# A two-layer decoder trunk: first x blocks on VectorE, later turns of q and k, h stored from SyncE

## The chip, the cores and the metric

The kernel runs on one core of one Trainium2 chip. The metric is the device time of one execution in microseconds (us). The engines are TensorE (PE, which multiplies), VectorE (DVE), ScalarE (ACT), GpSimd (POOL) and SyncE (SP, which here only issues transfers). ACT and POOL issue transfers too.

## The reference

Two layers of a decoder trunk for one sequence of 1024 positions and width 1024, in float32. Cut to what matters:

```python
proj = x @ w_in                      # 4864 columns
u_pool, q, k, v, xc, gate_b, gate_c, gate_logits = split(proj)
o_a = multiscale_pool_mixer(u_pool)                    # windows 2/4/8/16
q, k = apply_partial_rope(q, cos, sin), apply_partial_rope(k, cos, sin)
o_b = sliding_window_gqa_sinks(q, k, v, sinks)         # window 128
o_c = gate_b * causal_dwconv(gate_c * xc, conv_w)
merged = sum(sigmoid(gates[i]) * (o_i @ w_branch_i))
x = layer_norm(ALPHA * x + merged @ w_o)
up = causal_dwconv(x @ w_up, ffn_conv_w); a, b = split(up)
h = silu(a) * b                                        # 2816 columns
x = layer_norm(ALPHA * x + h @ w_down)
```

The rotary part turns the first 16 of each 64 head channels: x1*cos - x2*sin and x2*cos + x1*sin. cos and sin come from `positions`, the same for both layers.

## The kernel before

Every float32 product is made of three reduced-precision ones: a value is split into a high part (a cast, L90, on ACT) and the remainder (a subtraction, L94, on DVE or POOL), and `product` (L110, L111, L112) adds high x high, high x low and low x high in a PSUM bank. On top of that, matrices are cut into 2 x 2 blocks and multiplied with seven block products instead of eight, so differences of blocks of x and of the weights are needed.

A layer goes through four stages. `project` makes 19 **pairs** of column tiles of `w_in`: 12 of gate logits, and kv, two of q, two for the gated convolution, its second gate, and the pooled input. `merge` does attention and the branches, `output` the product with `w_o` and a norm. The **up** stage (`feed_forward`) makes 22 pairs of `w_up`; `activated` turns each into h and, for every odd f, makes the seven h blocks that the down product needs from the last two tiles (L790 to L793, POOL) and stores them to DRAM by seven transfers of 256 KB (L796, through `store`, L664, issued by POOL). `down` runs seven steps (A11, A12, S2, S1, S3, S4, A22) over 11 blocks j each, adds the results to y, norms the rows, and in the last layer writes them to `out`.

A `pair` has two parts. Its `begin` loads w0, runs two block products, and copies the first out of its bank (`u`, L700, ACT); its `rest` loads w1, makes weight differences on POOL (L713, L710), splits them, and runs five more products, with copies and additions between (T2's copy L724, T1's copy L728, DVE's L703, L730, L733, L735). Then it calls its `then`, the column's own work. `run_pairs` calls begin, `due`, rest for each pair in turn. `todo` is the list of pieces that wait for a pair's number (`due`), `pend` a list of pieces called by `pending`.

The first pair's x blocks are made in `first_loads`; its `rest` (L229) makes the differences T1 to T4 and the remainders, some on DVE and some on POOL. The rope angles go through DRAM: `rope_tables` writes rows (L177), `rope_spread` (L180) clears two tables, fills them from the rows, and writes them to DRAM (L192, L193), and `load_tables` (L926) loads them in each layer. `rotate` turns a tile: a copy on ACT (L339), four small transfers that ACT issues (L341, L342), three DVE operations (L343 to L345), and then `parts` splits it (L92, L94), all at once when the pair ends.

SP's and PE's instructions run in the order in which the code is written; on the other engines a scheduler orders them. An engine takes its instructions strictly in order, so a waiting one holds back those behind it. Tiles rotate through a few buffers by tag: X 14, t 6, s 3, pt 3, q 1, ql 1, ws 3, w 6.

Of the kernel before, what the change touches and what calls it, by code (L numbers as in the profile page):

```python
# [60 lines left out]
class Trunk:  # L61
# [118 lines left out]
    def rope_spread(self):  # L180
        nc, rows = self.nc, self.rows
        cos = self.new([P, S], F32, "t")
        sin = self.new([P, S], F32, "t")
        nc.vector.memset(cos, 1.0)
        nc.vector.memset(sin, 0.0)
        for base in (0, 64):
            for half in range(2):
                lo = base + 8 * half
                nc.sync.dma_start(cos[lo:lo + 8, :], rows[0])
                nc.sync.dma_start(sin[lo:lo + 8, :], rows[2 - half])  # L190
        self.tables = self.dram.tile([2, P, S], F32, name="rope_tables")
        nc.sync.dma_start(self.tables[0], cos[:])  # L192
        nc.sync.dma_start(self.tables[1], sin[:])  # L193

# [6 lines left out]
    def first_loads(self):  # L201
# [27 lines left out]
        def rest():  # L229
            self.new_blocks(("T2", "T1", "T3", "T4"))  # L230
            for j in range(2):
                x("B12", 0, 1, ("t", "q"), j)
                x("B22", 1, 1, ("t", "w"), j)
            put = lambda b, j, s, e: self.split(self.xc[b][0][:, 2 * j:2 * j + 2], self.xc[b][1][:, 2 * j:2 * j + 2],
                                                s, "scalar", e)
            g = lambda n, j: f[n, j][:]
            t1 = {}
            for j in range(2):
                t1[j] = self.new([P, 2, HALF], F32, "w")
                nc.vector.tensor_tensor(t1[j][:], g("B12", j), g("B11", j), op=ALU.subtract)  # L240
                nc.gpsimd.tensor_tensor(g("B12", j), g("B22", j), g("B12", j), op=ALU.subtract)
                nc.vector.tensor_tensor(g("B11", j), g("B22", j), t1[j][:], op=ALU.subtract)
                put("T2", j, g("B11", j), "vector")
                put("T1", j, t1[j][:], "gpsimd")
            for j in range(2):
                put("T3", j, g("B12", j), "vector")
            self.new_blocks(("B22",))
            for j in range(2):
                nc.vector.tensor_tensor(g("B21", j), g("B11", j), g("B21", j), op=ALU.subtract)
                put("T4", j, g("B21", j), "vector")  # L250
                put("B22", j, g("B22", j), "gpsimd")

# [82 lines left out]
    def rotate(self, c, cos, sin):  # L335
# [9 lines left out]
        nc.vector.tensor_tensor(c[:], c[:], swp[:], op=ALU.add)  # L345
        return self.parts(swp, c)

    def parts(self, hi, c):

        hi, lo = hi[:].bitcast(F32R), c[:].bitcast(F32R)  # L350
        self.split(hi, lo, c[:], "vector", "gpsimd")
        return hi, lo
# [16 lines left out]

    def project(self, l, tables, first):  # L370

        nc = self.nc
        st = {}

        def kv(k, v):
            st["tab"] = tables()
            hi, lo = self.rotate(k, *st["tab"])
            for n in range(2):
                own, other = slice(64 * n, 64 * n + 64), slice(64 - 64 * n, P - 64 * n)
                self.store(self.kd[n, own], hi[own])  # L380
                self.store(self.kd[n, other], lo[own])

# [10 lines left out]

            self.todo.append((self.pairs + 1, keys_first))

        def qq(i):
            def then(*c):
                for j in range(2):
                    for n, x in enumerate(self.rotate(c[j], *st["tab"])):
                        self.store(self.qd[:, :, n, 2 * i + j, :].rearrange("b c q -> c b q"),  # L400
                                   x.rearrange("c (b q) -> c b q", q=P))
            return then
# [16 lines left out]
        def gate_b(*c):  # L419
            for i in range(2):  # L420
                nc.vector.tensor_tensor(c[i][:], c[i][:], st["y", i][:], op=ALU.mult)
                operand(i, st["y", i], c[i])

        def pooled(*c):
            for i in range(2):
# [12 lines left out]

                self.todo.append((self.pairs + 2 + i, mapped))

# [6 lines left out]

        gates = [gate(n) for n in range(12)]
        thens = gates[:2] + [kv, qq(0), qq(1), gates[2], gated_conv(0), gated_conv(1), gate_b, gates[3], pooled] + gates[4:]
        made, second = first or (None, None)  # L450
        if second:
            self.pend.append(lambda: None)
            self.pend.append(lambda: (second(), self.parameters()))
            self.todo.append((1, self.rope_spread))
# [201 lines left out]
    def made(self, src, e_lo="vector"):  # L656
# [3 lines left out]
        return t[:, 0, :], t[:, 1, :]  # L660

    def store(self, dst, src):

        self.nc.gpsimd.dma_start(dst, src if src.dtype == F32 else src.bitcast(F32))  # L664

    def pair(self, srcs, parity, then, made=None):
# [38 lines left out]
        def rest():  # L705
            a, (ca, cb), u = st["a"], st["c"], st["u"]
            a11, a12 = st["w0"][:, lo], st["w0"][:, hi]
            w1 = load(1)
            a21, a22 = w1[:, lo], w1[:, hi]
            sub = lambda out, x, y: nc.gpsimd.tensor_tensor(out, x, y, op=ALU.subtract)  # L710
            s1 = self.new([P, HALF], F32, "ql")
# [52 lines left out]
    def activated(self, l, f, ca, cb):  # L764
# [30 lines left out]
        for name, src in blocks:  # L795
            self.store(four(self.hs[STATIONARY.index(name), f // 2]), src)  # L796

    def down(self, l):
# [78 lines left out]
        for n, (name, banks, fresh, closes, reads) in enumerate(plan):  # L877
            if n == 5:
                g, b = self.gains(l, 1)
            held = []  # L880
            for j in range(NJ):
                late = n == 6 and j >= NJ - (LATE if last else 6)
                ops = operands(n, name, j, late)
# [21 lines left out]
    def finish(self, l, t, y, g, b):  # L905
# [7 lines left out]
        elif t == 7:  # L913
            out = lambda cs: (nc.sync if cs.start else nc.scalar).dma_start(self.out[t, :, cs], z[:, cs])
            self.norm(z, g, b, "halves", None, out)
        else:
            self.norm(z, g, b, "vector")
            nc.sync.dma_start(self.out[t], z[:])

# [6 lines left out]
    def load_tables(self):  # L926
        cos, sin = self.new([P, S], F32, "q"), self.new([P, S], F32, "pt")
        self.nc.sync.dma_start(cos[:], self.tables[0])
        self.nc.sync.dma_start(sin[:], self.tables[1])
        return cos, sin  # L930

    def run(self):
        self.pend, self.todo, self.pairs = [], [], 0
        self.spill = self.dram.tile([8, P, D], F32, name="spill")
# [7 lines left out]
        with self.tc.manual_schedule(engines={mybir.EngineType.SP, mybir.EngineType.PE}):  # L942
# [10 lines left out]
            self.constants()  # L953
            self.rope_tables()
            for l in range(DEPTH):
                self.project(l, self.load_tables, first if l == 0 else None)
                self.merge(l)
# [18 lines left out]
def lay_out(inp):  # L976
# [10 lines left out]
    for l in range(DEPTH):  # L987
# [5 lines left out]
        gt = ac + [gbb[:, e * 256:(e + 1) * 256] for e in range(4)]  # L993
        win.append(column_tiles(np.concatenate([*gt[:2], k, v, q[:, heads], gt[2], *conv, gb, gt[3], u, *gt[4:]], axis=1)))
        a = column_tiles(inp["w_branch_a"][l])
# [45 lines left out]
```

## Time and profile before

| | |
|---|---|
| median of 3 runs | 2927.76 us (2921.65 to 3175.77) |
| the profiled execution | 2920.5 us, span 2918.7 us |
| busy: PE, DVE, POOL, ACT | 2614.4, 1974.0, 1552.7, 1196.5 us |
| mean granted clock of PE | 0.951 |
| moved by DMA | 390.64 MB, mean 134 GB/s |
| PE busy from 0 to 73, 73 to 146, 146 to 219 us | 34.90, 53.78, 56.00 us |

The profile is one execution on the chip. Rows of the timeline give start, duration, engine, line of the kernel, operation, output <- input and, in brackets, how long the engine was idle before and what ended that. Rows of waits give the waiting engine, tile and line, what it waited for, the sum in us, the number of times and the longest. SPq and ACTq are instructions that issue transfers.

### The profile page before, as it was taken

What the parts mean: (1) busy time and instruction counts of PE and PEld (TensorE: products, weight loads), DVE (VectorE), ACT (ScalarE), POOL (GpSimd) and SP (SyncE); (2) the same over time, 40 slices, a digit from 0 to 9 for tenths busy, and PEclk for the clock granted to TensorE, in tenths of its full rate; (3) what the DMA queues carried; (4) which work ended last, traced back from release to release, by engine and by line L of the source; (5) the groups of instructions that cost most, each with busy time, mean ns of one, the idle gap of its engine ahead of it and who ended that gap; (6) DMA issues with size and microseconds to landing.
All of it is one profiled execution on the core that took longest, in us unless ns stands there. A gap on an engine that the chain in (4) does not pass through costs nothing.

```text
span 2918.7 us, 31980 instructions
## 1 busy us (share of the span) xinstructions
PE 2614.4 (90%) x11408; PEld 2113.4 (72%) x11408; DVE 1974.0 (68%) x2285; ACT 1196.5 (41%) x1987; POOL 1552.7 (53%) x1103
## 2 busy tenths in 40 slices
PE   4779999999799999799689899999989999997985
PEld 3568887777677777678577788878767777776763
DVE  7476635846888888475486664377587888875754
ACT  4333444533444444334343335444344444443332
POOL 5354534766466666270644555367656666553513
PEclk7889999999999999999789999999989999998996
DMA  2342338554133222565323324665522322337533
GB/s 98 114 144 84 121 135 245 158 177 166 61 98 100 93 93 94 210 237 164 110 79 121 105 95 153 207 183 163 190 94 91 101 94 91 98 115 259 177 105 130
DMA packets 131184, 390.64 MB, mean 134 GB/s; under 512 B 17056, under 2 KB 17824, under 8 KB 130000
## 3 DMA queue, kind: packets, MB, share of 16 engines
q1 hardware_dynamic: 93872, 258.41, 27.2%
q0 software_dynamic: 25856, 90.85, 10.2%
q10 hardware_dynamic: 11296, 39.35, 3.5%
q8 instruction: 89, 1.46, 0.2%
q14 instruction: 71, 0.58, 0.1%
HBM read 282.79 MB, written 104.43 MB: 133 GB/s over the span
## 4 chain that ended last, share of the span: by engine, by line
PE 25%; DVE 20%; POOL 13%; DMA 8%; issue 7%; ACT 4%; SPq 0%; ACTq 0%; POOLq 0%; DVEq 0%
PE b L111 8%; PE b L112 8%; PE b L110 8%; POOL ws L710 5%; DVE w L94 5%; DMA ws<-in_w_up 4%; DVE q L775 4%; POOL ql L713 2%; ACT w L90 1%; DVE t L733 1%; DVE ve L274 1%; POOL X L836 1%; DMA X<-in_w_down 1%; ACT q L772 1%; PE b L297 1%
## 5 line engine op out<-in xcount | busy, mean ns | idle before, releaser
L110 PE MATMUL b<-X,w 128*128 128x512 f32 x2552 | 1020.9, 400 | 122.0 <-ACT s L700 62.5
L112 PE MATMUL b<-X,w 128*128 128x512 f32 x2552 | 1004.4, 394 | 23.5 <-DVE w L94 15.2
L111 PE MATMUL b<-X,w 128*128 128x512 f32 x2552 | 1004.1, 393 | 2.0 <-DVE X L94 2.0
L94 DVE TENSOR_TENSOR w<-ws,w 128x512 fp32r<-128x512 f32 (+1 forms) x449 | 508.4, 1135 | 321.2 <-ACT w L90 314.2
L110 PEld LDWEIGHTS b<-X,w 128*128 128x128 f32 x2552 | 485.8, 190 | 259.0 <-ACT s L700 79.8
L90 ACT CAST w<-ws 128x512 fp32r<-128x512 f32 (+1 forms) x605 | 405.8, 680 | 491.4 <-POOL ws L710 200.2
L112 PEld LDWEIGHTS b<-X,w 128*128 128x128 f32 x2552 | 485.0, 190 | 131.7 <-DVE w L94 18.1
L111 PEld LDWEIGHTS b<-X,w 128*128 128x128 f32 x2552 | 486.7, 191 | 101.0 <-DVE X L94 3.4
L94 POOL TENSOR_TENSOR w<-ws,w 128x512 fp32r<-128x512 f32 (+2 forms) x156 | 305.6, 1961 | 407.4 <-ACT w L90 404.4
L713 POOL TENSOR_TENSOR ql<-ws 128x512 f32<-128x512 f32 x82 | 119.0, 1452 | 348.6 <-DMA ws<-in_w_in 216.9
L110 PE MATMUL b<-w 128*128 128x512 f32 x528 | 209.7, 397 | 53.9 <-ACT w L90 53.9
L111 PE MATMUL b<-w,w 128*128 128x512 f32 x528 | 211.8, 401 | 26.2 <-DVE w L94 20.4
L112 PE MATMUL b<-w,w 128*128 128x512 f32 x528 | 208.5, 395 | 0.0
L94 DVE TENSOR_TENSOR w<-X,w 128x512 fp32r<-128x512 f32 (+1 forms) x106 | 111.6, 1073 | 90.3 <-ACT w L90 84.8
L775 DVE SCALAR_TENSOR_TENSOR q<-t,par,q 128x1023 f32<-128x1023 f32 x88 | 153.4, 1743 | 13.8 <-ACT q L772 13.6
L110 PEld LDWEIGHTS b<-w 128*128 128x128 f32 x528 | 101.2, 192 | 77.5 <-ACT w L90 56.0
L710 POOL TENSOR_TENSOR ws<-ws,ws 128x512 f32<-128x512 f32 x82 | 153.2, 1868 | 5.8
L111 PEld LDWEIGHTS b<-w,w 128*128 128x128 f32 x528 | 101.1, 192 | 56.8 <-DVE w L94 30.1
L775 DVE SCALAR_TENSOR_TENSOR pt<-t,par,pt 128x1023 f32<-128x1023 f32 x88 | 135.6, 1541 | 0.3
L710 POOL TENSOR_TENSOR ws<-ql,ws 128x512 f32<-128x512 f32 x82 | 128.7, 1569 | 6.3
L90 ACT CAST w<-X 128x512 fp32r<-128x512 f32 (+1 forms) x110 | 75.4, 704 | 134.9 <-PE b L112 64.4
L710 POOL TENSOR_TENSOR ws<-ws 128x512 f32<-128x512 f32 x82 | 116.2, 1417 | 14.7 <-DVE w L94 11.7
(247 smaller groups left out, 3892.6 us busy)
## 6 DMA issues: line engine op xcount, KB each, us to landing
ws<-in_w_up SPq DMA_DIRECT2D x88, 512.0 KB
ws<-in_w_in SPq DMA_DIRECT2D x75, 512.0 KB
gates<-t ACTq DMA_DIRECT2D x48, 512.0 KB
h_blocks<-t POOLq DMA_DIRECT2D x88, 256.0 KB, 2.8
ws<-in_w_o SPq DMA_DIRECT2D x40, 512.0 KB
h_blocks<-pt POOLq DMA_DIRECT2D x66, 256.0 KB, 2.7
t<-gates SPq DMA_DIRECT2D x32, 512.0 KB
t<-q_parts POOLq DMA_DIRECT2D x64, 256.0 KB, 4.4
```

Of the source, the lines that this page charges most:

```text
L90: self.nc.scalar.copy(hi, src)
L94: return eng.tensor_tensor(lo, src, hi.bitcast(F32), op=ALU.subtract)
L110: self.nc.tensor.matmul(out, wh, xh, start=start and i == 0, stop=False, skip_group_check=more)
L111: self.nc.tensor.matmul(out, wh, xl, start=False, stop=False, skip_group_check=more)
L112: self.nc.tensor.matmul(out, wl, xh, start=False, stop=stop and i == n - 1, skip_group_check=more)
L274: nc.vector.scalar_tensor_tensor(ve[:], ve[:], r[:], r[:], op0=ALU.mult, op1=ALU.mult)
L297: self.nc.tensor.transpose(ps[:, k * P:(k + 1) * P], src[:, k * P:(k + 1) * P], self.ident[:])
L710: sub = lambda out, x, y: nc.gpsimd.tensor_tensor(out, x, y, op=ALU.subtract)
L713: nc.gpsimd.tensor_tensor(s1[:], a21, a22, op=ALU.add)
L733: nc.vector.tensor_tensor(part(cb, 0), flat(v[:, 1, :]), flat(d[:]), op=ALU.subtract)
L772: nc.scalar.mul(y[:], c[:], w(2))
L775: nc.vector.scalar_tensor_tensor(y[:, d:], c[:, :S - d], w(k), y[:, d:], op0=ALU.mult, op1=ALU.add)
```

## The change

1. First x blocks: the differences for T3 and the remainders of T1 and B22, made by POOL before, are made by DVE, in another order. POOL does none of the x blocks.
2. Rope tables: `rope_spread` uses the q and pt buffers instead of two t buffers and keeps the tables there for layer 0 (`self.tab`); the copy in DRAM for layer 1 is written from POOL. In the code the call that makes the angles comes after the second load of x.
3. Columns: gate columns alternate with the others (g0, g1, kv, g2, q0, g3, q1, g4, conv0, g5, conv1, g6, gate_b, g7, pooled, g8 to g11), with the weights laid out to match. k and q are turned (`rotate`) one pair later and split and stored two pairs later; the high part is cast by ACT instead of DVE. The split of gate_b's product comes a pair later.
4. h blocks: for f below 20 the seven stores are put off to pair f + 2 and issued by SP right behind that pair's w1 load. f = 21 is stored by POOL as before; what is left of the others goes in `down`, at j = 3 of its first step.
5. Down: the pieces of `pend` come at other places in A22, and the last layer's stores of even rows go there instead of being issued at once.

```diff
 def rope_spread(self):
-    cos = self.new([P, S], F32, "t")
-    sin = self.new([P, S], F32, "t")
+    cos, sin = self.new([P, S], F32, "q"), self.new([P, S], F32, "pt")
...
-    nc.sync.dma_start(self.tables[0], cos[:])
-    nc.sync.dma_start(self.tables[1], sin[:])
+    nc.gpsimd.dma_start(self.tables[0], cos[:])
+    nc.gpsimd.dma_start(self.tables[1], sin[:])
+    self.tab = cos, sin
...
 # first_loads, rest
-    nc.gpsimd.tensor_tensor(g("B12", j), g("B22", j), g("B12", j), op=ALU.subtract)
...
-    put("T1", j, t1[j][:], "gpsimd")
+for j in range(2):
+    put("T1", j, t1[j][:], "vector")
 for j in range(2):
+    nc.vector.tensor_tensor(g("B12", j), g("B22", j), g("B12", j), op=ALU.subtract)
     put("T3", j, g("B12", j), "vector")
...
-    put("B22", j, g("B22", j), "gpsimd")
+    put("B22", j, g("B22", j), "vector")
...
 # project
+def later(n, f):
+    self.todo.append((self.pairs + n, f))
+def turn(c, put):
+    free = []
+    later(1, lambda: free.append(self.rotate(c, *self.tab)))
+    later(2, lambda: put(*self.parts(free[0], c)))
...
-thens = gates[:2] + [kv, qq(0), qq(1), gates[2], gated_conv(0), gated_conv(1), gate_b, gates[3], pooled] + gates[4:]
+others = [kv, qq(0), qq(1), gated_conv(0), gated_conv(1), gate_b, pooled]
+thens = gates[:1] + [f for i in range(7) for f in (gates[i + 1], others[i])] + gates[8:]
...
 # parts
-    self.split(hi, lo, c[:], "vector", "gpsimd")
+    self.split(hi, lo, c[:], "scalar", "gpsimd")
...
+def put_off(self, dst, src):
+    self.late.append((self.pairs + 2, dst, src))
+def flush(self, all=False):
+    for n, dst, src in [x for x in self.late if all or x[0] <= self.pairs]:
+        self.nc.sync.dma_start(dst, src)
+    self.late = [] if all else [x for x in self.late if x[0] > self.pairs]
...
 # pair, rest, behind w1's load
+    self.flush()
...
 # activated
-    self.store(four(self.hs[STATIONARY.index(name), f // 2]), src)
+    (self.put_off if f < NFF - 2 else self.store)(four(self.hs[STATIONARY.index(name), f // 2]), src)
...
 # down
+    if n == 0 and j == 3:
+        self.flush(True)
...
-    if n == 6 and j in (3, 4):
+    if n == 6 and j == 4:
         self.pending()
...
-    if held and q < 2:
-        self.pending()
+    if held and q < 3:
+        self.pending(4 if last else 1)
...
 # finish, last layer
-    nc.sync.dma_start(self.out[t], z[:])
+    put = lambda: nc.sync.dma_start(self.out[t], z[:])
+    if t % 2:
+        put()
+    else:
+        self.pend.append(put)
```

Where instructions stand now, at three places. The first is SP in the third and fourth pair of layer 0; `in_w_in` are pair loads, `rope_rows` and `rope_tables` the angles in DRAM. Before:

```order
L190 DMA t_542<-rope_rows 8x1024
L192 DMA rope_tables<-t_541 128x1024
L193 DMA rope_tables<-t_542 128x1024
L680 DMA ws_556<-in_w_in 128x1024
L928 DMA q_647<-rope_tables 128x1024
L929 DMA pt_648<-rope_tables 128x1024
L680 DMA ws_666<-in_w_in 128x1024
```

After the change, in the same place:

```order
L188 DMA q_541<-rope_rows 8x1024
L189 DMA pt_542<-rope_rows 8x1024
L704 DMA ws_556<-in_w_in 128x1024
L704 DMA ws_647<-in_w_in 128x1024
```

The four transfers of whole tables are gone from between the loads. The eight `rope_rows` stay on SP; the clears for which they wait moved on DVE from behind the work of pair 1 (L703 of t_538) to ahead of pair 1's weight remainders.

The second is ACT in the pair behind the first q column, in which q's two tiles (t_844, t_845) are turned. L340 is the copy of `rotate`, L342 and L343 its transfers, L724 the copy `u` (L700 before), L749 T2's copy (L724 before) and L753 T1's (L728 before). After the change:

```order
L342 DMA pt_983<-t_844 8x1024
L724 COPY s_966<-b_952 128x512
L343 DMA pt_983<-t_844 8x1024
L342 DMA pt_983<-t_844 8x1024
L343 DMA pt_983<-t_844 8x1024
L342 DMA pt_992<-t_845 8x1024
L753 COPY s_1050<-b_1023 128x512
L343 DMA pt_992<-t_845 8x1024
L342 DMA pt_992<-t_845 8x1024
L343 DMA pt_992<-t_845 8x1024
L90 CAST w_1020<-ws_944 128x512
L749 COPY s_966<-b_952 128x512
```

Before, the turn of the first q column stands in the pair that follows it like this:

```order
L339 COPY pt_827<-t_703 128x1024
L700 COPY s_862<-b_848 128x512
L341 DMA pt_827<-t_703 8x1024
L342 DMA pt_827<-t_703 8x1024
L341 DMA pt_827<-t_703 8x1024
L342 DMA pt_827<-t_703 8x1024
L90 CAST w_898<-ws_840 128x512
L724 COPY s_862<-b_848 128x512
```

The copy of `u` stands ahead of most of the transfers now, and T2's copy (L749) behind T1's (L753), three transfers and a cast, where before it came ahead of T1's.

The third is SP at the end of the last layer; `out` is the result, the lines with `h_blocks` and `in_w_down` are the two halves of a down operand. Before:

```order
L842 DMA X_20476<-in_w_down 128x512
L918 DMA out<-pt_19222 128x1024
L918 DMA out<-pt_19226 128x1024
L918 DMA out<-t_19230 128x1024
L918 DMA out<-t_19234 128x1024
L819 DMA s_20571<-h_blocks_15683 128x512
L845 DMA s_20571<-in_w_down 128x512
```

After:

```order
L867 DMA X_20472<-in_w_down 128x512
L844 DMA s_20563<-h_blocks_15679 128x512
L870 DMA s_20563<-in_w_down 128x512
L844 DMA ws_20583<-h_blocks_15679 128x512
L870 DMA ws_20583<-in_w_down 128x512
```

The four stores of even rows now come behind all eleven A22 operands.

More of the change, by code (lines that the diff above doesn't have):

```diff
@@ L345, in rotate @@
         nc.vector.tensor_tensor(c[:], c[:], swp[:], op=ALU.add)
-        return self.parts(swp, c)
+        return swp
     def parts(self, hi, c):
         hi, lo = hi[:].bitcast(F32R), c[:].bitcast(F32R)
-        self.split(hi, lo, c[:], "vector", "gpsimd")
+        self.split(hi, lo, c[:], "scalar", "gpsimd")
         return hi, lo
@@ L368, in windows, with project, put @@
                                        op0=ALU.mult, op1=ALU.subtract)
-    def project(self, l, tables, first):
+    def project(self, l, first):
         nc = self.nc
         st = {}
-        def kv(k, v):
[L376 to L381, printed above, removed]
+        def later(n, f):
[4 more added lines that the diff above has]
+            later(2, lambda: put(*self.parts(free[0], c)))
+        def kv(k, v):
+            if l:
+                self.load_tables()
+            def put(hi, lo):
+                for n in range(2):
+                    own, other = slice(64 * n, 64 * n + 64), slice(64 - 64 * n, P - 64 * n)
+                    self.store(self.kd[n, own], hi[own])
+                    self.store(self.kd[n, other], lo[own])
             def keys_first():
@@ L392, in keys_first @@
                     self.store(self.vd[:, :, c * HALF:(c + 1) * HALF].rearrange("a p c -> p a c"), t)
-            self.todo.append((self.pairs + 1, keys_first))
+            later(1, keys_first)
+            turn(k, put)
         def qq(i):
@@ L398, in then, with put @@
                 for j in range(2):
-                    for n, x in enumerate(self.rotate(c[j], *st["tab"])):
-                        self.store(self.qd[:, :, n, 2 * i + j, :].rearrange("b c q -> c b q"),
-                                   x.rearrange("c (b q) -> c b q", q=P))
+                    def put(*x, j=j):
+                        for n in range(2):
+                            self.store(self.qd[:, :, n, 2 * i + j, :].rearrange("b c q -> c b q"),
+                                       x[n].rearrange("c (b q) -> c b q", q=P))
+                    turn(c[j], put)
             return then
@@ L421, in gate_b @@
                 nc.vector.tensor_tensor(c[i][:], c[i][:], st["y", i][:], op=ALU.mult)
-                operand(i, st["y", i], c[i])
+                later(1, lambda i=i: operand(i, st["y", i], c[i]))
         def pooled(*c):
@@ L437, in mapped @@
                     operand(2 + i, self.new([P, S], F32, "pt"), c[i])
-                self.todo.append((self.pairs + 2 + i, mapped))
+                later(2 + i, mapped)
         def gate(n):
@@ L452, in project @@
             self.pend.append(lambda: None)
-            self.pend.append(lambda: (second(), self.parameters()))
+            self.pend.append(lambda: (second(), self.rope_tables(), self.parameters()))
             self.todo.append((1, self.rope_spread))
@@ L929, in load_tables @@
         self.nc.sync.dma_start(sin[:], self.tables[1])
-        return cos, sin
+        self.tab = cos, sin
     def run(self):
-        self.pend, self.todo, self.pairs = [], [], 0
+        self.pend, self.todo, self.late, self.pairs = [], [], [], 0
         self.spill = self.dram.tile([8, P, D], F32, name="spill")
@@ L953, in run @@
             self.constants()
-            self.rope_tables()
             for l in range(DEPTH):
-                self.project(l, self.load_tables, first if l == 0 else None)
+                self.project(l, first if l == 0 else None)
                 self.merge(l)
@@ L993, in lay_out @@
         gt = ac + [gbb[:, e * 256:(e + 1) * 256] for e in range(4)]
-        win.append(column_tiles(np.concatenate([*gt[:2], k, v, q[:, heads], gt[2], *conv, gb, gt[3], u, *gt[4:]], axis=1)))
+        qs = q[:, heads]
+        some = [np.concatenate([k, v], axis=1), qs[:, :256], qs[:, 256:], np.concatenate(conv[:2], axis=1),
+                np.concatenate(conv[2:], axis=1), gb, u]
+        mixed = gt[:1] + [m for i in range(7) for m in (gt[i + 1], some[i])] + gt[8:]
+        win.append(column_tiles(np.concatenate(mixed, axis=1)))
         a = column_tiles(inp["w_branch_a"][l])
```

## The prediction

> **What bounds the kernel now.** I read the busy totals and the clock in 40 slices first, then what TensorE (PE) waits for, then four stretches in order of time.
>
> ```profile
> PE 2614.4 (90%) x11408; PEld 2113.4 (72%) x11408; DVE 1974.0 (68%) x2285; ACT 1196.5 (41%) x1987; POOL 1552.7 (53%) x1103
> PEclk7889999999999999999789999999989999998996
> PE b L110 <- ACT w L90: 99.2, 11, 24.9
> PE b L110 <- ACT s L700: 62.5, 41, 8.0
> ```
>
> PE is the bound: 90% busy. About 304 us are not busy, so a change that leaves the matmuls alone can win only there. The two rows of waits (engine, tile, line, what it waited for: us in total, times, longest) hold half of it: few long waits for a weight's cast (L90), and 41 short ones for the copy of the first product out of its bank (L700). The change touches both. The span is 2918.7, this execution took 2920.5, and the runs shown have the median 2927.76; I sum against 2920.5 and leave 7 us of that spread to the range.
>
> **Part 1: first x blocks.** The rows are start, duration, engine, line, and in brackets the idle time before and its releaser.
>
> ```profile
> 25.95 1.22 DVE L240 TENSOR_TENSOR w<-t,pt 128x1024 f32<-128x1024 f32 x1
> 28.34 3.38 DVE L240 TENSOR_TENSOR w<-q,pt 128x1024 f32<-128x1024 f32 x1
> 39.34 2.39 DVE L150 TENSOR_SCALAR sink<-sink 128x8 f32<-128x8 f32 x2
> 46.08 2.28 DVE L94 TENSOR_TENSOR X<-pt,X 128x1024 fp32r<-128x1024 f32 x1
> 57.07 0.68 DVE L94 TENSOR_TENSOR w<-ws,w 128x512 fp32r<-128x512 f32 x1
> 57.80 0.80 PE L112 MATMUL b<-X,w 128*128 128x512 f32 x1 [8.61 <-DVE w L94]
> ```
>
> DVE does 12 large operations from 25.95 to 57.07, most at 2.28 to 3.38 us, which I put down to POOL's work on x beside it; the first takes 1.22. PE's L112 at 57.80 waits for the weight remainder that stands behind them. Afterwards DVE does 18 of them and POOL none. 18 x 1.22 = 22.0, plus the sink rows 2.4, gives 50.3; POOL's four weight subtractions (L713, L710) now fall into this time, and if each catches one DVE operation (2.28 instead of 1.22) that adds 4.2: 54.5. I take 52.5, between the ends, so L112 starts at 53: **+5 us** (+3 to +7). POOL reaches those subtractions earlier, so the 24.9 us wait ahead of this one turns partly into a longer one here; only the end counts.
>
> **Part 2: the rope rows on SyncE (SP).**
>
> ```profile
> SPq L189 <- DVE t L184: 32.7, 1, 32.7
> 92.92 0.91 DVE L184 MEMSET t<- 128x1024 f32 x1 [0.16 <-issue]
> 93.90 0.35 SPq L189 DMA_DIRECT2D t<-rope_rows  x1
> 103.99 12.20 SPq L680 DMA_DIRECT2D ws<-in_w_in  x3
> 106.50 1.26 POOL L713 TENSOR_TENSOR ql<-ws 128x512 f32<-128x512 f32 x1 [30.28 <-DMA ws<-in_w_in]
> 111.15 0.80 PE L110 MATMUL b<-X,w 128*128 128x512 f32 x1 [19.19 <-ACT w L90]
> ```
>
> SP stands 32.7 us at L189 until DVE clears the tables, which stands behind pair 1's last work on DVE; then come twelve table transfers, and the next w1 load goes at 103.99. POOL, idle since 76.2, gets it at 106.50 and PE loses 19.19. The two clears now stand ahead of pair 1's remainders on DVE (0.91 each, up to 2 us, hidden behind PE's 19 us pair; I charge 0.8), in buffers that are free, and L192, L193, L928, L929 leave SP. So SP goes on at about 60, and the load waits only for its buffer, free around POOL's 76. What is late next is nothing in this pair: **+18.4** (+15 to +21). That the angles stand behind the second load in the code counts nothing: their rows on DVE keep their place.
>
> 111.15 also shows a matmul of 0.80, and the first two slices of the clock row are 7 and 8. The Trainium skill ("TensorE: Matmul & The Clock Gate", Part 1) says that the array falls to half clock after an idle window and climbs back after steady work; by that rule some 2 us of slow steps behind the stall would go as well. The trace agrees with the slow steps; the sum leaves them out.
>
> **Part 3: turning k and q.** Rows five and six are PE's waits from 140 to 220 and from 1580 to 1660; the last is a stretch: length, PE busy (count), PEld, DVE, ACT, POOL, clock, DMA share, GB/s.
>
> ```profile
> 152.92 1.04 ACT L339 COPY pt<-t 128x1024 f32<-128x1024 f32 x1 [4.73 <-DMA k_parts<-pt]
> 153.99 0.63 ACTq L341 DMA_DIRECT2D pt<-t  x1
> 158.32 0.58 ACT L700 COPY s<-b 128x512 f32<-128x512 f32 x1
> PE b L110 <- ACT s L700: 17.0, 3, 7.4
> PE b L110 <- ACT s L700: 16.6, 3, 8.0
> 219.00:438.00 219.00, 219.00 (x968) 181.39 (x967) 119.28 (x134) 93.31 (x152) 106.19 (x78) 1.00 0.33 114
> ```
>
> Here ACT waits for a pt buffer that a store still reads, and PE's next copy L700 is queued behind. With the turn a pair later, its store two pairs later and gate columns between, the buffers are free by then, so these 33.6 us go. But in the four pairs in which q is turned (two a layer) ACT's new order sets T2's copy (L724) behind T1's (L728), three DMA issues and a cast. T3 cannot start before: 0.59 + 3 x 0.63 + 0.62 + 0.59 = 3.7 us after T1, say 4. 33.6 - 4 x 4 = **+17.6** (+5, if waits for pt come back in other pairs, to +30, if the copy in fact comes early). The extra gate's and pooled's later place: the pooled maps now fall where the projection ends, and PE is full there before (219.00 of 219.00, 968 matmuls at 0.226 us a step), so a loss is possible and a gain is not: **-2** (-8 to 0).
>
> **Part 4: storing h in the up stage.** The first row is the stretch of layer 0's up pairs.
>
> ```profile
> 781.00:1160.00 379.00, 362.04 (x1549) 287.84 (x1549) 327.44 (x280) 171.41 (x263) 245.69 (x196) 1.00 0.30 95
> 948.49 2.32 POOL L710 TENSOR_TENSOR ws<-ws,ws 128x512 f32<-128x512 f32 x1
> 968.42 2.32 POOL L710 TENSOR_TENSOR ws<-ws,ws 128x512 f32<-128x512 f32 x1
> 977.47 1.80 POOL L664 DMA_DIRECT2D h_blocks<-t  x3
> 989.40 2.32 POOL L710 TENSOR_TENSOR ws<-ws,ws 128x512 f32<-128x512 f32 x1
> 959.48 1.28 DVE L775 SCALAR_TENSOR_TENSOR q<-t,par,q 128x1023 f32<-128x1023 f32 x1 [0.62 <-ACT q L772]
> 978.20 3.48 DVE L775 SCALAR_TENSOR_TENSOR q<-t,par,q 128x1023 f32<-128x1023 f32 x1
> 962.92 1.14 ACT L90 CAST w<-ws 128x512 fp32r<-128x512 f32 x2
> 943.23 41.23 SPq L680 DMA_DIRECT2D ws<-in_w_up  x5
> ```
>
> Clock 1.00, DVE 86% busy, 17 us of PE idle in this layer. POOL's L710 starts 19.93 us after the last in one kind of pair and 20.98 in the other, the one with the store instructions. There DVE's first L775 takes 3.48 instead of 1.28 while POOL issues three of them, and the copy that frees PE's bank is late with it. Taking seven issues from POOL should make the long pairs like the short ones: 1.05 x 10 a layer x 2 = **+21**. Ends: 8, if POOL's arithmetic (L790 to L793) is what holds DVE; 35, if the short pairs shorten too (84 matmuls at 0.226 need 19.0). SP takes 7 issues of 0.3 to 0.5 us a double pair and waits most of a pair, so they are hidden unless their transfers delay the w0 load behind them (rival D). The pt buffer that is held longer is wanted by ACT's L772 only at the end of pair f+2.
>
> **Part 5: the end.**
>
> ```profile
> 2802.19 0.43 SPq L842 DMA_DIRECT2D X<-in_w_down  x1
> 2842.50 3.66 SPq L918 DMA_DIRECT2D out<-pt  x2
> 2850.07 0.41 SPq L819 DMA_DIRECT2D s<-h_blocks  x1
> 2854.59 1.26 POOL L846 TENSOR_TENSOR s<-X,s 128x512 f32<-128x512 f32 x1 [28.05 <-DMA s<-in_w_down]
> 2856.98 0.80 PE L110 MATMUL b<-w 128*128 128x512 f32 x1 [23.13 <-ACT w L90]
> 2847.26 2.36 DVE L291 TENSOR_TENSOR t<-t,t 128x1024 f32<-128x1024 f32 x2 [0.70 <-ACT t L290]
> 2891.11 0.69 DVE L860 TENSOR_TENSOR pt<-pt,b 128x512 f32<-128x512 f32 x1 [1.31 <-PE b L112]
> ```
>
> SP issues nothing from 2802 to 2842: the out stores of four rows wait for their norms, and the eleven A22 loads stand behind them. PE loses 23.13, then runs at the pace of operands made one at a time until the first row's last read at 2891.11. Now the loads stand ahead, so they land while PE still works on S4, whose end is 2856.98 - 23.5 = 2833.5. A22's three early columns need 3 x 4 x 3 x 0.226 = 8.1 us of PE, the eight held ones 5.4 for the first row: at best 2847. But DVE's norms run until 2849.6 and hold back the remainder of the third column: 2849.6 + 2.1 for it + 2.7 for its matmuls + 5.4 = 2860, say 2862. Gain 2891 - 1.3 - 2862 = **+28** (+22 with another operand 6 late; +36 if the norms give way). The three rows behind stay as they are.
>
> The end of layer 0's down stage gets its transposes in other places, and the load of y behind the last h stores stays: **+3** (-5 to +8).
>
> **Sum.** 5 + 18.4 + 17.6 - 2 + 21 + 28 + 3 = 91: 2920.5 - 91 = **2829**. All low ends together would give 2880, all high ones 2790.
>
> **Rivals.**
> A, the forecast (0.63): 2806 to 2852.
> B, more (0.12): even pairs drop towards 19.0 and the end takes its upper price: 91 + 14 + 8 gives 2807 or less, down to 2795.
> C, less (0.17): ACT's new order costs more than 4 us a place, waits for pt return in gate pairs and the norms eat half of the end: 91 - 12 - 13 - 14 gives 2868, 2853 to 2885.
> D, slower (0.06): the seven stores, 7 x 256 KB = 1.84 MB, stand on SP ahead of the next w0 load, and if the queue drains them in turn that load is late. w1 goes at 943.2 and w0's cast is due at about 962.9: 19.7 us, less eight issues of 0.4, for the stores and w0's 0.52 MB, which is 143 GB/s.
>
> ```profile
> 438.00:511.00 73.00, 66.55 (x317) 56.28 (x316) 38.04 (x79) 34.52 (x95) 33.12 (x35) 0.91 0.87 245
> h_blocks<-t POOLq DMA_DIRECT2D x88, 256.0 KB, 2.8
> ```
>
> Against it: a stretch of 73 us moves 245 GB/s. For it: one store takes 2.8 from issue to landing; seven one after another and w0, twice a store's size, are 25.2, 5.5 over, in 20 pairs 110 lost against 70 won elsewhere: 2920.5 + 110 - 70 = 2960. It decides as soon as the queue drains slower than 143 GB/s. "DMA: Bandwidth & Descriptors" of the Trainium skill (Queues, rings and completion order) says that SP's descriptors are consumed in ring order on each engine, which is the rule against this change; the trace has no store and load behind one another on SP to show it.
> E (0.02): the changed parts cancel, 2900 to 2935.
>
> **How the numbers follow.** A measurement of this kernel tells about 2% from no change, so faster means below 2869. A and B lie there, and most of C: 0.63 + 0.12 + 0.10 = 0.85. Within 2% are the rest of C, E and a mild D: 0.10. Slower 0.05. The range 2802 to 2868 leaves out half of B, a third of C, D and E: about 0.2.
>
> **What would show it.** Part 1: POOL's first L713 before 40 and PE's L112 near 53. Part 2: no wait of 32 us of SP for the clears, PE full from 60 to 150. Part 3: no L700 wait over 2 us in the projection, four waits of 4 us for L724's copy. Part 4: L710 starts near 19.9 apart in all pairs, the DVE row of 3.48 gone. Part 5: SP's A22 loads before 2833 on the old count, and DVE's first last read 28 us earlier against the end of S4. Wrong it would be if w0's cast in the up stage waits for its transfer, or if new waits for pt or s buffers stand in the gate pairs.

## The result and the profile after

The median of four runs is 2818.94 us (2816.18 to 2819.78). The kernel before took 2921.49 to 2927.76 in three runs, 2923.6 in the mean; its fourth, 3175.77, is disturbed and not part of the ratio. The ratio is 0.964, with a 95% interval of 0.9621 to 0.9659: some 105 us less, where 91 were forecast. The profiled execution took 2816.18 us, with a span of 2814.4, which is 104.3 shorter than the span before.

First the page, and the longest of PE's waits, in the kernel after the change. L724 is the copy of the first product (L700 before), L749 that of T2's product (L724 before).

```profile
PE 2596.4 (92%) x11408; PEld 2118.0 (75%) x11408; DVE 1876.6 (67%) x2273; ACT 1228.1 (44%) x2005; POOL 1466.5 (52%) x959
PEclk7989999999999999999799999999999999998998
PE b L110 <- ACT w L90: 45.2, 10, 15.8
PE b L110 <- ACT s L724: 18.5, 7, 4.4
PE b L110 <- ACT s L749: 17.5, 6, 3.5
```

The waits for a cast fell from 99.2 to 45.2 and those for the first copy from 62.5 to 18.5; a new row has come in, L749 with 17.5, which the prediction priced at four times 4 us (six such waits came, of 3.5 at most). PE has the same 11408 matmuls. DVE's busy time fell by 97 us with 12 instructions less.

**The start.** The two rows at the end are stretches: length, busy time of PE (with its matmuls), PEld (its weight loads), DVE, ACT, POOL, clock, DMA share, GB/s.

```profile
33.74 2.28 DVE L94 TENSOR_TENSOR X<-pt,X 128x1024 fp32r<-128x1024 f32 x1
49.57 1.21 DVE L94 TENSOR_TENSOR X<-w,X 128x1024 fp32r<-128x1024 f32 x1
50.71 0.23 DVE L150 TENSOR_SCALAR sink<-sink 128x8 f32<-128x8 f32 x2
51.59 0.80 PE L112 MATMUL b<-X,w 128*128 128x512 f32 x1 [11.56 <-DVE w L94]
55.09 0.35 SPq L188 DMA_DIRECT2D q<-rope_rows  x1
65.70 38.68 SPq L704 DMA_DIRECT2D ws<-in_w_in  x6
0.00:73.00 73.00, 41.25 (x157) 32.67 (x158) 47.80 (x62) 33.66 (x48) 26.90 (x35) 0.79 0.37 131
73.00:146.00 73.00, 71.15 (x317) 58.38 (x315) 33.42 (x43) 31.14 (x50) 29.84 (x25) 1.00 0.36 118
```

DVE's operations take 2.28 while POOL makes its four subtractions, and 1.21 once it is idle. PE's held L112 starts at 51.59 instead of 57.80. SP issues the rope rows from 55.09 instead of 93.90, and PE is busy for 71.15 of the second 73 us, 53.78 before, at full clock. Counted by matmuls, the one that started at 132.6 before starts at 104.5. Ahead of it one wait of 19.19 is gone, and with it slow steps: before, the ten matmuls behind that wait took 4.83 us (111.15 to 115.98, most of them 0.43 apart); the same ten now take 2.27, 0.23 apart.

**The projection.** First the waits of PE from 110 to 240, then ACT in the pair in which the first column of q is turned.

```profile
PE b L110 <- ACT s L724: 8.8, 3, 3.9
PE b L110 <- ACT s L749: 6.8, 2, 3.5
143.72 1.99 ACT L340 COPY pt<-t 128x1024 f32<-128x1024 f32 x2 [2.14 <-DVE t L760]
145.62 0.58 ACT L724 COPY s<-b 128x512 f32<-128x512 f32 x1
153.67 0.59 ACT L753 COPY s<-b 128x512 f32<-128x512 f32 x1 [7.47 <-PE b L112]
155.02 0.63 ACTq L343 DMA_DIRECT2D pt<-t  x1
155.69 0.62 ACT L90 CAST w<-ws 128x512 fp32r<-128x512 f32 x1 [1.44 <-DMA pt<-t]
156.21 0.58 ACT L749 COPY s<-b 128x512 f32<-128x512 f32 x1
```

The old waits of 17.0 for the first copy are not gone: 8.8 are left, and 6.8 have come for T2's copy. The turn's copies (L340) start as soon as q's last block is written (L760), though the code calls the turn a pair later, and L724 stands behind both.

**The up stage.** The first row is the same 379 us of layer 0's pairs; SP rows follow, then what SP waited for.

```profile
749.00:1128.00 379.00, 375.12 (x1651) 309.22 (x1650) 300.77 (x297) 189.50 (x278) 228.13 (x140) 1.00 0.34 104
886.77 2.15 POOL L735 TENSOR_TENSOR ws<-ws,ws 128x512 f32<-128x512 f32 x1
905.94 2.16 POOL L735 TENSOR_TENSOR ws<-ws,ws 128x512 f32<-128x512 f32 x1
925.55 1.63 POOL L735 TENSOR_TENSOR ws<-ws,ws 128x512 f32<-128x512 f32 x1
895.95 2.12 DVE L800 SCALAR_TENSOR_TENSOR q<-t,par,q 128x1023 f32<-128x1023 f32 x1
915.24 1.28 DVE L800 SCALAR_TENSOR_TENSOR q<-t,par,q 128x1023 f32<-128x1023 f32 x1 [0.61 <-ACT q L797]
895.73 23.59 SPq L704 DMA_DIRECT2D ws<-in_w_up  x4
919.37 6.18 SPq L683 DMA_DIRECT2D h_blocks<-pt  x3
SPq L683 <- DVE pt L804: 86.3, 20, 5.5
SPq L683 <- POOL t L815: 68.0, 18, 4.2
```

PE's idle time in this stretch fell from 17 to 4 us. Both kinds of pair are now as long as PE's own work, 38.0 us for two (SP's loads at 857.75 and 895.73). DVE's 3.48 is 2.12. And SP does not store long after h is made, though the code says two pairs later: it runs so far ahead that it stands at the stores until h (L804) and its differences (L815) are there.

**The end.** SP, DVE and PE in order of time.

```profile
2750.68 0.43 SPq L870 DMA_DIRECT2D ws<-in_w_down  x1
2775.47 1.48 SPq L945 DMA_DIRECT2D out<-pt  x2
2776.68 1.16 DVE L94 TENSOR_TENSOR w<-X,w 128x1024 fp32r<-128x1024 f32 x1
2777.90 0.80 PE L111 MATMUL b<-w,w 128*128 128x512 f32 x1 [9.19 <-DVE w L94]
2788.38 0.69 DVE L885 TENSOR_TENSOR pt<-pt,b 128x512 f32<-128x512 f32 x1 [2.80 <-PE b L112]
```

SP has all A22 operands issued by 2751, ahead of the stores to out. The wait of 23.13 is gone; 9.19 are left, for the remainder that stands behind the norms on DVE.

Where the 104 us between the two profiled executions came from, by the time of the same matmul in the two traces (us gained):

| stretch | layer 0 | layer 1 |
|---|---|---|
| start, to the end of the third pair's work | 28.1 | - |
| rest of the projection | -3.2 | -3.4 |
| merge and output product | 6.5 | 2.3 |
| up stage | 23.9 | 24.7 |
| down | 3.1 | 22.4 |

### The profile page after: what moved, and what is told of

Its sections match the earlier page's. It is cut to its first block, busy times and chain, and to the rows that moved or that the text cites. A ratio compares the mean times of both kernels' runs of the same rounds, so it can differ in the third digit from the quotient of the medians.

```text
span 2814.4 us, 31939 instructions
## 1 busy us (share of the span) xinstructions
PE 2596.4 (92%) x11408; PEld 2118.0 (75%) x11408; DVE 1876.6 (67%) x2273; ACT 1228.1 (44%) x2005; POOL 1466.5 (52%) x959
## 4 chain that ended last, share of the span: by engine, by line
PE 31%; DVE 7%; issue 4%; POOL 4%; ACT 2%; DMA 2%; SPq 0%; ACTq 0%; DVEq 0%; POOLq 0%
PE b L111 10%; PE b L112 10%; PE b L110 10%; DVE w L94 1%; DVE X L94 1%; ACT s L507 1%; DVE ve L275 1%; ACT w L90 0%; POOL ws L735 0%; POOL X L861 0%; POOL w L94 0%; ACT X L90 0%; POOL X L863 0%; DVE st L259 0%; DVE m L498 0%
## 5 line engine op out<-in xcount | busy, mean ns | idle before, releaser
L110 PE MATMUL b<-X,w 128*128 128x512 f32 x2552 | 1016.4, 398 | 56.9 <-ACT s L724 18.5
L112 PE MATMUL b<-X,w 128*128 128x512 f32 x2552 | 1009.6, 396 | 27.6 <-DVE w L94 19.3
L94 DVE TENSOR_TENSOR w<-ws,w 128x512 fp32r<-128x512 f32 (+1 forms) x449 | 466.8, 1043 | 357.4 <-ACT w L90 342.9
L112 PEld LDWEIGHTS b<-X,w 128*128 128x128 f32 x2552 | 487.9, 191 | 135.7 <-DVE w L94 22.5
L94 POOL TENSOR_TENSOR w<-ws,w 128x512 fp32r<-128x512 f32 (+1 forms) x156 | 307.4, 1973 | 427.5 <-ACT w L90 425.3
L738 POOL TENSOR_TENSOR ql<-ws 128x512 f32<-128x512 f32 x82 | 125.2, 1527 | 348.9 <-DMA ws<-in_w_in 256.5
L111 PE MATMUL b<-w,w 128*128 128x512 f32 x528 | 215.3, 408 | 37.4 <-DVE w L94 29.6
L112 PE MATMUL b<-w,w 128*128 128x512 f32 x528 | 211.6, 401 | 0.0
L735 POOL TENSOR_TENSOR ws<-ws,ws 128x512 f32<-128x512 f32 x82 | 141.8, 1729 | 5.9
L800 DVE SCALAR_TENSOR_TENSOR q<-t,par,q 128x1023 f32<-128x1023 f32 x88 | 126.8, 1441 | 16.2 <-ACT q L797 15.1
L800 DVE SCALAR_TENSOR_TENSOR pt<-t,par,pt 128x1023 f32<-128x1023 f32 x88 | 122.1, 1388 | 0.3
```

The source lines that it names most:

```text
L94: return eng.tensor_tensor(lo, src, hi.bitcast(F32), op=ALU.subtract)
L110: self.nc.tensor.matmul(out, wh, xh, start=start and i == 0, stop=False, skip_group_check=more)
L111: self.nc.tensor.matmul(out, wh, xl, start=False, stop=False, skip_group_check=more)
L112: self.nc.tensor.matmul(out, wl, xh, start=False, stop=stop and i == n - 1, skip_group_check=more)
L738: nc.gpsimd.tensor_tensor(s1[:], a21, a22, op=ALU.add)
L800: nc.vector.scalar_tensor_tensor(y[:, d:], c[:, :S - d], w(k), y[:, d:], op0=ALU.mult, op1=ALU.add)
```

## Experiments: each part undone or done alone

Each kernel was timed beside the kernel before; the ratios below are to it.

**only_h_late**: the kernel before, with `put_off`, `flush` and the lines that use them; one of these is shown.

```diff
-    self.store(four(...), src)
+    (self.put_off if f < NFF - 2 else self.store)(four(...), src)
```

> The kernel before with part 4 alone (h stores put off two pairs and issued by SP). Theory: POOL's store instructions lengthen all pairs of the up stage, and the whole gain of its two stretches, 23.9 + 24.7 = 48.6 us between the two traces, belongs to part 4: 2924.7 - 48.6 = 2876, pairs 19.0 us apart. Rival, the step on record: only the pairs with stores shorten, 21 us: 2904, pairs 19.9 apart.

Measured: 2873.79 us, ratio 0.9838 (0.9824 to 0.9853): 47 us less. The theory's 2876 holds, the 21 us on record don't. The stretch of the up pairs and the page of this kernel:

```profile
780.00:1159.00 379.00, 375.16 (x1644) 309.02 (x1643) 301.02 (x296) 189.21 (x278) 226.68 (x140) 1.00 0.33 103
PE 2602.2 (91%) x11408; PEld 2123.3 (74%) x11408; DVE 1888.8 (66%) x2285; ACT 1212.5 (42%) x1987; POOL 1483.2 (52%) x963
```

PE is full here as well, and the 140 store instructions that left POOL took 85 us of DVE's busy time with them (1974.0 to 1888.8), with the same 2285 DVE instructions.

**late_pool**: the changed kernel, with the put-off stores issued by POOL.

```diff
-    self.nc.sync.dma_start(dst, src)
+    self.nc.gpsimd.dma_start(dst, src)
```

> The changed kernel with the put-off stores issued by POOL instead of SP, at the same place of the program. Theory: it matters which engine issues them, so the up stage goes back to 20.4 us a pair and the time to 2819 + 40 to 50 = 2859 to 2869. Rival: it matters that they come late and no longer stand between the weight subtractions and the h blocks: within 8 us of 2819.

Measured: 2873.67 us, ratio 0.9843 (0.9826 to 0.9859), 55 us more than the change. The stretch of the up pairs, and POOL and DVE in one of them:

```profile
750.00:1129.00 379.00, 362.22 (x1547) 288.80 (x1546) 327.80 (x278) 170.17 (x261) 241.72 (x194) 1.00 0.30 95
905.33 1.78 POOL L683 DMA_DIRECT2D h_blocks<-t  x3
906.98 1.45 POOL L735 TENSOR_TENSOR ws<-ws 128x512 f32<-128x512 f32 x1
906.03 3.48 DVE L800 SCALAR_TENSOR_TENSOR q<-t,par,q 128x1023 f32<-128x1023 f32 x1
```

The stretch is that of the kernel before to within 0.2 us of PE, and DVE's row of 3.48 is back. The stores stand between the subtractions on POOL again, because the scheduler orders POOL. So a later place in the code wins nothing on POOL, and the gain needs another engine to issue the stores; a version with late stores on POOL in an order of one's own wasn't tried.

**early_sp**: put off by one pair.

```diff
-    self.late.append((self.pairs + 2, dst, src))
+    self.late.append((self.pairs + 1, dst, src))
```

> The changed kernel with the stores put off by one pair instead of two, still on SP. In the trace SP runs more than a pair ahead, and w0's cast is done about 14 us before PE needs it. Theory: SP takes its instructions in order, so the loads of pair f+2 now stand behind stores whose h is not made yet; w0 would be issued some 18 us later, 4 more than its lead plus its landing and splitting, about 5.5 us lost in each of 20 pairs: 2819 + 110 = 2929. Rival: SP has slack enough, since it waits most of each pair anyway: 2819.

Measured: 3012.02 us, ratio 1.0312 (1.0293 to 1.0331). This is the rival D of the prediction come true in another way: 193 us more than the change, 9.7 in each of 20 pairs, where 5.5 were expected.

SP's rows, what SP waited for, and ACT's cast of a w0:

```profile
944.61 23.49 SPq L683 DMA_DIRECT2D h_blocks<-pt  x3
968.28 3.06 SPq L683 DMA_DIRECT2D h_blocks<-t  x4
971.44 21.41 SPq L704 DMA_DIRECT2D ws<-in_w_up  x4
SPq L683 <- DVE pt L804: 428.6, 21, 22.2
975.24 0.62 ACT L90 CAST w<-ws 128x512 fp32r<-128x512 f32 x1 [3.99 <-DMA ws<-in_w_up]
```

SP stands up to 22.2 us at a store until h is made, and four loads go behind it. The late cast also stands ahead of ACT's work on h, which delays the next h: that loop is my reading of why it is more than 5.5, and it was not measured by itself. Part of the loss is the clock: it is 0.95 from 760 to 1200, in the up stage of layer 0, and 1.00 in that of the change, an estimated 22 us of these 440. One pair's difference in the program decides between 105 us won and 91 lost.

The trace also answers what the prediction left open in rival D. The w0 load that SP issues at 971.44, 0.4 us behind the last of seven stores, is cast from at 975.24: at most 3.8 us from issue to landing, against 3.4 to 3.6 for three loads of this size in the up stage of the kernel before. Six of the seven stores and the load were issued from 966.90 on and took 8.3 us up to the cast, where the sum's prices would give 6 x 2.8 + 5.6 = 22.4.

**columns_before**: part 3 undone.

```diff
...
-thens = gates[:1] + [f for i in range(7) for f in (gates[i + 1], others[i])] + gates[8:]
+thens = gates[:2] + [kv, qq(0), qq(1), gates[2], gated_conv(0), gated_conv(1), gate_b, gates[3], pooled] + gates[4:]
...
-later(1, lambda: free.append(self.rotate(c, *self.tab)))
-later(2, lambda: put(*self.parts(free[0], c)))
+put(*self.parts(self.rotate(c, *self.tab), c))
...
```

> The changed kernel with part 3 undone (columns in the old order, k and q turned and split when their pair ends). By the step on record, part 3 is worth 17.6 - 2 = 15.6 us, so undoing it gives 2834.5. By the two traces the projections lost 3.2 and 3.4 us against the old order, and the merges behind them became 6.5 and 2.3 us shorter: part 3 is worth 2 us or nothing, 2817 to 2822, and the waits for the first copy are back with 17 us in each projection.

Measured: 2820.22 us, ratio 0.9654 (0.964 to 0.9668), which cannot be told from the change's 0.964. Part 3 wins nothing that can be told (1 us by the medians, 5 by the profiled executions), not 15.6. PE's waits from 110 to 220 in this kernel:

```profile
PE b L110 <- ACT s L722: 17.4, 3, 8.2
```

17.4 against 8.8 + 6.8 after the change. The rest of the projection is 4 us shorter here and the merge with the output product 4.8 longer (297.5 against 292.7); why it gains from the new order I did not separate.

**both_urgent**: the changed kernel, with the first copy and T2's raised in priority in every pair (`urgent` tells the scheduler to put an instruction ahead; T1's copy has it already). Only ACT's order changes (and what follows from it).

```diff
-    nc.scalar.copy(u[:, 0, :], a[:])
+    with self.urgent():
+        nc.scalar.copy(u[:, 0, :], a[:])
...
-    nc.scalar.copy(u[:, 1, :], a[:])
+    with self.urgent():
+        nc.scalar.copy(u[:, 1, :], a[:])
```

> The changed kernel with the copies of the first and of T2's product (L724, L749) at the same raised priority that T1's copy has, so that in the pairs in which q is turned T2's copy stands ahead of T1's and of three transfers. Theory: the four waits of 3.5 us for it go, 14 us: 2805 to 2808. Rival: the same transfers then hold back the cast for the last product or the next pair's copy, and the time stays within 4 us of 2819.

Measured: 2800.53 us, ratio 0.9583 (0.9568 to 0.9598): 18.4 less than the change (14.9 between the profiled executions), more than the 14 of the theory. The first row is ACT, the next two are PE's waits from 110 to 240; the last two are this stretch in the changed kernel and in this one.

```profile
149.98 0.59 ACT L751 COPY s<-b 128x512 f32<-128x512 f32 x1 [3.11 <-DMA pt<-t]
PE b L112 <- DVE w L94: 6.4, 4, 2.4
PE b L110 <- ACT s L725: 2.2, 2, 1.7
110.00:240.00 130.00, 114.21 (x455) 91.59 (x454) 75.60 (x70) 49.65 (x76) 62.13 (x45) 0.91 0.39 119
110.00:240.00 130.00, 121.38 (x513) 97.72 (x513) 75.43 (x79) 54.05 (x85) 67.11 (x49) 0.97 0.40 127
```

T2's copy (L751 here) goes 2.7 us ahead of T1's (152.70), and 15.6 us of waits for copies are 2.2; 6.4 for DVE's remainders have come in. The waits fall by 7 us only, yet the rest of the projection of layer 0 is 13.2 shorter (317.5 against 330.7). Most of the difference is the clock, 0.97 instead of 0.91 in this stretch: from the third pair's end on, the next 564 matmuls have 15 steps of 0.43 us where the change has 42, and the usual step is 0.23. Merge and output product take 8.6 us of it back (301.3 against 292.7).

**columns_urgent**: columns_before and the same two copies raised.

```diff
 # columns_before, and
+    with self.urgent():
     nc.scalar.copy(u[:, 0, :], a[:])
...
+    with self.urgent():
     nc.scalar.copy(u[:, 1, :], a[:])
```

> Part 3 undone and both copies raised: does the new column order gain anything once the copies no longer stand behind the turn? Theory: yes, because in the old order ACT's first copy of each turn still waits for a pt buffer that a store reads, with the raised copy behind it; only the second half of the 35 us of waits goes, 2820 - 12 = 2808, against 2800.5 in the new order. Rival: with the copies ahead both orders are alike: 2800 to 2803.

Measured: 2816.43 us, ratio 0.964 (0.9625 to 0.9654). The theory's direction holds, its size doesn't: raising the copies wins 4 us in the old order and 18 in the new one. So part 3 does pay, some 16 us (2800.53 against 2816.43), but only with the copies ahead.

**x_on_pool**: part 1 undone (the old lines of first_loads).

```diff
-    put("T1", j, t1[j][:], "vector")
+    put("T1", j, t1[j][:], "gpsimd")
...
-    nc.vector.tensor_tensor(g("B12", j), g("B22", j), g("B12", j), op=ALU.subtract)
+    nc.gpsimd.tensor_tensor(g("B12", j), g("B22", j), g("B12", j), op=ALU.subtract)
...
-    put("B22", j, g("B22", j), "vector")
+    put("B22", j, g("B22", j), "gpsimd")
```

> The changed kernel with part 1 undone (T3's differences and the remainders of T1 and B22 on POOL). PE's held matmul stood at 57.80 before and 51.59 after: 6.2 us, the step on record says 5. So 2824 to 2825. Rival: the matmuls behind it wait for other remainders and the start is the same: 2819.

Measured: 2826.98 us, ratio 0.968 (0.9658 to 0.9702); the interval touches that of the change, so the times alone hardly tell the two apart (8 us by the medians). In its trace the third pair's work ends 6.5 us later, and PE's waits at the start are the old ones (8.6 for the remainder, 24.8 for the cast). I take 6.5 as the part's price.

**tables_on_sp**: part 2 undone.

```diff
-    cos, sin = self.new([P, S], F32, "q"), self.new([P, S], F32, "pt")
+    cos = self.new([P, S], F32, "t")
+    sin = self.new([P, S], F32, "t")
...
-    nc.gpsimd.dma_start(self.tables[0], cos[:])
-    nc.gpsimd.dma_start(self.tables[1], sin[:])
+    nc.sync.dma_start(self.tables[0], cos[:])
+    nc.sync.dma_start(self.tables[1], sin[:])
...
-    if l:
-        self.load_tables()
+    self.load_tables()
```

> The changed kernel with part 2 undone (t buffers for the two tables, their copies written by SP and loaded again for layer 0). By the step on record 18.4; by the two traces the third pair ends 28.1 us earlier, of which 6.2 belong to the first x blocks, so 21.9: 2837 to 2841, with SP standing some 30 us at the rope rows. Rival: with k turned a pair later the tables are wanted a pair later too, and the loads fit in: 2822.

Measured: 2842.37 us, ratio 0.9735 (0.9716 to 0.9754), 23 us more. By the trace the third pair ends 21.2 us later, and SP's long wait is back:

```profile
SPq L189 <- DVE t L184: 32.3, 1, 32.3
```

PE's wait is back too, with 18.1 us, and the ten matmuls behind it take 4.83 again, 2.6 more than in the change. The two together are all but 0.5 of the 21.2.

**out_at_once**: the even rows' stores as before; the other places of `pend` stay as changed.

```diff
-    if t % 2:
-        put()
-    else:
-        self.pend.append(put)
+    nc.sync.dma_start(self.out[t], z[:])
```

> The changed kernel with the last layer's even rows stored to out at once, as before (the places of the pending pieces stay as changed). Theory: SP then stands at the out stores again while the A22 loads wait behind; the stretch between the up stage and the last matmul was 22.4 us shorter in the trace of the change, so 2819 + 22 = 2841, with one wait of PE of about 23 us. By the step on record 28: 2847. Rival: the A22 loads wait for their own buffers anyway and the norms set the end: 2819 to 2824.

Measured: 2846.53 us, ratio 0.9743 (0.9727 to 0.9759), 27.6 more than the change; its profiled execution, the fastest of its four (2843.37), is 22.7 longer from the up stage's end to the end of the span. SP's rows and PE's longest wait in it:

```profile
2763.95 3.66 SPq L945 DMA_DIRECT2D out<-pt  x2
2771.53 0.41 SPq L844 DMA_DIRECT2D s<-h_blocks  x1
PE b L110 <- ACT w L90: 23.1, 1, 23.1
```

The old picture: the loads behind the stores, PE waiting 23.1.

**end_urgent**: the split of A22's operands raised ahead of the norms.

```diff
+    with self.urgent() if last and n == 6 else ExitStack():
         self.split(wh, wl, st[:], "scalar", "gpsimd" if n > 4 and j % 2 else "vector")
```

> The changed kernel with the splitting of A22's operands in the last layer raised ahead of the norms. Theory: what is left of the wait at the end (9.2 us for a remainder that stands behind the norms of the even rows on VectorE) goes, and the norms fit beside the matmuls of the held columns: 2819 - 9 = 2810. Rival: the norms are then late by as much, and the last row's chain with them: 2819 or more.

Measured: 2817.1 us, ratio 0.9642 (0.9627 to 0.9658): no difference that can be told. In its trace the wait of 9.2 is 2.1 and the last 974 matmuls take 262.9 us instead of 270.1, but the stretch from the last matmul to the end of the span is 14.0 instead of 10.1: over half of what PE wins, the norms that are now late give back, as the rival said. The other 3 us went in stretches that this edit doesn't touch.

**y_later**: the loads of y in the first step of down moved behind the last column.

```diff
-    if n == 0 and j == 6:
+    if n == 0 and j == NJ - 1:
         for t in range(8):
```

> The changed kernel with the eight loads of y in the first step of down moved from behind j = 6 to behind the last column j = 10. Theory: the waits of 13 us between up and down in both layers come from SP standing at the loads of y until the last h blocks are read, with four operands behind; they go, 2819 - 26 = 2793. Rival: the last column's h block is itself made that late, so the wait only moves to it, some 3 us are won: 2813.

Measured: 2801.03 us, ratio 0.9583 (0.9567 to 0.9599), 18 less than the change: between theory (26) and rival (6). The wait of 12.9 in the first step of down is 2.5, among PE's waits from 1120 to 1240:

```profile
PE b L111 <- DVE w L94: 5.0, 7, 2.4
PE b L110 <- ACT w L90: 2.5, 1, 2.5
```

Counted by matmuls, 15.4 us are won at that wait in layer 0 and 17.0 in layer 1, but 7.4 and 6.5 are lost again in the down stage behind it. What that second loss waits for was not followed up.

**all_three**: both_urgent, end_urgent and y_later together.

> The changed kernel with both copies raised, A22's splitting raised and the loads of y moved. If the three are independent their gains add up: 2819 - 18.4 (measured for the copies) - 9 - 26 = 2766. If the loads of y only move the wait: 2786.

Measured: 2781.6 us, ratio 0.9522 (0.9506 to 0.9538). It beats both kernels, and the sum of the three measured gains (18.4 + 1.8 + 17.9, from 2818.9) gives 2780.8: they add up, within 1 us.

## Why the prediction was right, point by point

The time and its direction were right: 2819 against 2829, inside the range. The terms for the start and the ends came out near their prices, but of the two others one was 16 us too high and one 26 to 34 too low. That they cancelled in part is luck, and the closeness of the sum says little for its working. (All high ends together are 137 us, which gives 2783.5 and not 2790.)

- **First x blocks, +5**: right, 6.2 at the held matmul, 6.5 in the undo. POOL's four subtractions did slow four operations of DVE. The sink rows, which I charged 2.4, took 0.23: the 2.39 before were not their work.
- **Rope rows, +18.4**: right in mechanism, low in size: 21.2 in the undo. What is missing are the slow steps behind the stall, which the sum left out: the ten matmuls from 111.15 take 4.83 us before and 2.27 after, 2.6 us, and the clock of the second 73 us went from 0.86 to 1.00. The Trainium skill's rule ("TensorE: Matmul & The Clock Gate", Part 1), with which the prediction put this at some 2 us, agrees with that.
- **Turning k and q, +17.6, and -2 for the gates' places**: wrong, next to nothing instead of 15.6. The step that failed is that with the turn a pair later "these 33.6 us go". The code's later place is not ACT's later place: the scheduler puts the turn's copies where their data is ready, ahead of the first copy. T2's wait, priced at 3.7, was right (3.5 at most). With ACT's order put right, the part is worth about 16.
- **Storing h, +21**: right engine and right cause, wrong size: 47 to 55. The failing step is that long pairs become "like the short ones"; the short ones shortened too, to PE's own 19.0. This was rival B's mechanism, and the upper bound of 35 was too low: by the rows it stood on, (0.93 + 1.98) x 10 x 2 = 58 was there to be had (pairs 19.93 and 20.98 apart, against 19.0 of PE's own).
- **Rival D**: the budget counted from the issue of w1 and took h as ready. In fact SP reaches the stores before h is made. The loads behind were still early enough; by one pair less they aren't. The rule of the Trainium skill that was weighed against the change ("DMA: Bandwidth & Descriptors", Queues, rings and completion order) is about descriptors in a ring; what the runs show is SP itself in order, waiting. Of a cost of the ring order early_sp shows next to nothing: the load right behind the stores is there after at most 3.8 us, where three loads in the kernel before took 3.4 to 3.6.
- **The end, +28**: 22.4, and right in mechanism. The norms held back a remainder as foreseen, but until 2777.84, which is 2859.8 on the old count (the up stage ends 82.0 us earlier now), where I had 2851.7: S4's own last reads begin 11 us later on that count (2761.22 against 2831.85). Of these, 6.9 are PE's: in S4 it waits 3.5 us for operands, 2.0 of them for a remainder of POOL, where before it waited for nothing, and then runs at steps of 0.43. I put this down to the same engines splitting A22's operands beside S4's; that was not tested.
- **End of layer 0's down, +3**: 3.1, by the two traces alone; no run undoes it. The merges' 6.5 and 2.3 weren't foreseen.

## What to carry to other kernels

On engines that a scheduler orders, moving a piece of work later in the code does not by itself move it later on the engine; look at the order, and raise the one copy that the bottleneck waits for. Transfers that a busy engine issues between its arithmetic can cost more than their issue time, as here: give them to an engine that waits anyway, but put them in its order behind the loads that are wanted first, since an engine that waits for data holds back all that follows. Where several parts are changed at once, undo them one by one: here a part worth 0 and one worth twice its price looked like a good forecast.

## What the runs showed of the hardware

POOL's store instructions slow DVE far beyond the 1.05 us a pair that their place in the order suggests: without 140 of them DVE's 2285 instructions took 85 us less (only_h_late), 0.6 us for each store, and with them back on POOL DVE's 2273 took 91 us more (1967.4 in late_pool, 1876.6 in the change).

The same DVE operation took 3.48 us, 2.12 and 1.28. The 1.28 is beside neither stores nor arithmetic of POOL. The 2.12 (895.95, in the change) is beside a subtraction of POOL that runs from 895.24 to 896.98, and ends 1.1 us behind it. The Trainium skill ("SBUF — State Buffer", Who interferes with whom) says that a VectorE operation with two inputs in SBUF and a GpSimd operation that reads SBUF exclude each other, and that the second to issue waits; the 2.12 fits that. The 3.48 (906.03, in late_pool) does not follow from it: the subtraction beside it starts 0.95 us after DVE's operation, which still ends 1.1 us behind the subtraction's end, while three stores run from 905.33 to 907.11, across the start of both. That the stores hold DVE back until POOL's next operation is through is my reading; how they do it no run here shows.

A wait of PE costs more than its length where the clock falls: behind the wait of 19.19 ten matmuls took 4.83 us instead of 2.27, and in both_urgent the projection of layer 0 won 13 us with 7 us of waits less.
